# A merge moved behind the next unit's values, and two gate steps that work out of SBUF

## The chip, the cores and the metric

The kernel runs on one core of a Trainium2 chip. The metric is the device time of one execution in microseconds (us). The core's engines each work through a queue of their own: TensorE (PE in the profile, with PEld for its weight loads), VectorE (DVE), ScalarE (ACT), GpSimd (POOL) and SyncE (SP), which here only issues DMAs.

## The reference, cut to what matters

One layer of a decoder with 512 tokens, width 1024. One RMSNorm feeds one projection; half of its columns go to an attention with three branches (compressed blocks, selected blocks, window), half to a gated short convolution.

```python
h = rms_norm(x, norm_w); proj = h @ w_in
# attention, per block of 128 queries, 8 heads:
p_c = masked_softmax(q @ kc + bias);  o_c = p_c @ vc      # compressed keys, values
o_s = masked_softmax(q @ ks + bias) @ vs                  # selected blocks (here: all)
o_w = masked_softmax(q @ kw + bias) @ vw                  # window
attn = g0 * o_c + g1 * o_s + g2 * o_w
conv = conv_b * conv3(conv_c * conv_h)
mixed = concat([attn * silu(z_attn), conv * silu(z_conv)])
out = rms_norm(x + mixed @ w_out, final_norm_w)
```

## The kernel before, in words

Matrix products that need more than the engine's single pass split each operand into a high part and a rest and add three products (hi*hi, hi*lo, lo*hi). The high part of a weight is cast on ACT, the rest is subtracted on POOL.

**Order.** The order on TensorE is that of the program. ACT, DVE, POOL and the DMAs of SP are ordered by the compiler's planner, which takes what is ready in its own timeline; each engine then executes its queue strictly in that order. So the order on these four can change wherever the program changes.

**Units.** The attention is cut into 14 units: query blocks in the order 3, 2, 0, 1 (`BLOCKS`), each with two head groups (jj = 0, 1). A unit has `scores()` (products into the four PSUM banks `S`, L872; bias and maximum on DVE, L763; exponent on ACT, L881; weights on ACT L899 and DVE L900; a transposing DMA into `pt`, L902) and `values()` (L838 with `pt` and `V`, summed in a PSUM bank `o`, of which there are two). Block 0 has two units, 8 and 9, each with both the selected and the window branch; all others have one branch.

**The compressed branch.** Its scores are computed along with the first branch of each group (`fused`), its weights for all heads of a block at once in `Compressed.weigh()`, after the scores of the block's second group: DVE L807 to L814, POOL L818, ACT L819, POOL L820, and a transposing DMA into `ptc` (L822). `Group.merge()` adds the compressed branch to the group's bank `o` (L838 with `ptc`) and multiplies the bank into `za`, the gate (DVE L846).

**The loop.** In the loop at the end (L939 to L951) step n runs the values of unit n-2, the merge where its group is complete, the scores of unit n, and then fills TensorE with other tasks for a given cost (`st.fill`, 35 products of 512 columns, each counted as 216 ns, in the steps of blocks 0 and 1). At n = 10 all 27 projection tasks are completed first (`BEHIND`); behind them the fill consists of the product with the second half of the output matrix (`conv_out_task`: `pc`, L441 to L445, bank by bank `tb` in two PSUM banks `proj`, taken out by DVE L448) and of the casts and subtractions of the first half (`woa_task`, ACT L465, POOL L467).

**Gate chunks.** The projection tasks `za0` to `za3` and `zc0` to `zc3` end in `silu_to`: a multiplication by R in the PSUM bank (`normed`, DVE L274), a tanh on ACT (L281), a last step on DVE (L282), and for `zc` one more multiplication by R on POOL (L284). The bank is one of the two `proj` banks, 24 products fill it.

Of the kernel before, what the change touches and what calls it, by code (L numbers as in the profile page):

```python
# [9 lines left out]
F32 = mybir.dt.float32  # L10
# [3 lines left out]
AF = mybir.ActivationFunctionType  # L14
ALU = mybir.AluOpType
# [3 lines left out]
S = 512  # L19
# [67 lines left out]
def hybrid_kernel(ctx: ExitStack, tc: tile.TileContext, xt0, xt, x, ws, wt, wv, w1k, w1v, cst, rbr, wo, fnw, out):  # L87
    nc = tc.nc
    ctx.enter_context(tc.manual_schedule(engines={mybir.EngineType.PE}))
    one = ctx.enter_context(tc.tile_pool(name="one", bufs=1))  # L90
# [181 lines left out]
    def normed(ps):  # L272

        nc.vector.tensor_mul(ps, ps, R)  # L274
        return ps

    def silu_to(dst, conv=False):
        def evac(ps):

            normed(ps)  # L280
            nc.scalar.activation(dst(), ps, AF.Tanh, scale=0.5)  # L281
            nc.vector.scalar_tensor_tensor(out=dst(), in0=dst(), scalar=1.0, in1=ps, op0=ALU.add, op1=ALU.mult)  # L282
            if conv:
                nc.gpsimd.tensor_mul(dst(), dst(), R)  # L284
        return evac
# [305 lines left out]
    R = one.tile([128, S], F32, name="R")  # L591
# [68 lines left out]
    with tc.manual_schedule(engines={mybir.EngineType.Activation, mybir.EngineType.DVE, mybir.EngineType.Pool}):  # L660
# [4 lines left out]
        for k in range(8):  # L665
            if k % 2 == 0:
# [5 lines left out]
                                           op0=ALU.mult, op1=ALU.subtract)  # L672
# [241 lines left out]
    units, cmps = [], {qb: Compressed(qb) for qb in range(4)}  # L914
# [24 lines left out]
    for n in range(2, len(units) + 2):  # L939
        st.run(BEHIND.get(n, 0))  # L940
        u = units[n - 2]
        u.values()
        if 1 in u.brs:
            u.gr.merge()
        if n < len(units):
            units[n].scores()
            st.fill(FILL[units[n].gr.qb])
        elif n == len(units):

            st.run(len(st.tasks) - 2)  # L950
            st.fill(2700)  # L951
# [60 lines left out]
```

## Time and profile before

| what | before |
|---|---|
| time, median of 3 runs (lowest, highest) | 282.04 us (280.89, 282.22) |
| time of the profiled execution, its span | 282.41 us, 280.2 us |
| PE busy, PEld busy | 262.9 us (94%), 213.3 us (76%) |
| DVE, ACT, POOL busy | 180.7 us (65%), 151.6 us (54%), 145.2 us (52%) |
| mean granted TensorE clock | 0.976 |

The span runs from the first to the last instruction of one profiled execution; busy times are sums over the engine's instructions. The granted clock is the share of full speed that TensorE was given. All places in time are us from the start of the span. Idle time of an engine that nobody waits for costs nothing.

### The profile page before, as it was taken

The page shows a single profiled execution, that of the slowest core. Times are in us where ns is not written, and L with a number is a line of the kernel's source. Part 1 is how long each engine was busy: PE and PEld are TensorE (multiplying, and loading weights), DVE is VectorE, ACT ScalarE, POOL GpSimd, SP SyncE. Part 2 cuts the span into 40 slices and gives each one's busy share as a digit, 9 for nine tenths or more (in the row PEclk, how much of TensorE's full clock was granted, in tenths as well). Part 3 has the DMA queues.
Part 4 walks back from the last instruction along what each step waited for, and adds up shares of the span by engine and source line. Part 5 has one row for each costly group of instructions (what it writes and reads, how often), then busy time and mean ns, then how long its engine had stood idle before and what let it go on. Part 6 is the DMA issues. An engine that isn't in the chain of part 4 may idle for free. (4 is left out here: it accounts for less than half of the span.)

```text
span 280.2 us, 4423 instructions
## 1 busy us (share of the span) xinstructions
PE 262.9 (94%) x1488; PEld 213.3 (76%) x1488; DVE 180.7 (65%) x481; ACT 151.6 (54%) x342; POOL 145.2 (52%) x143
## 2 busy tenths in 40 slices
PE   7999999999999799999999999999990999999990
PEld 7888998878878578787878787878870867778780
DVE  5761937979766348663687854395990758758462
ACT  4973735577538356462727365538276516518542
POOL 5776596749341725636474947554648810005300
PEclk9999999999999999999999999999996699999997
DMA  6999997307944816947374688871929041352323
GB/s 200 392 287 271 211 220 273 106 0 219 198 185 88 195 57 148 210 102 196 80 160 102 152 229 206 202 210 20 207 51 253 34 78 37 75 152 39 112 102 122
DMA packets 57677, 43.29 MB, mean 155 GB/s; under 512 B 47288, under 2 KB 48568, under 8 KB 57656
## 3 DMA queue, kind: packets, MB, share of 16 engines
q1 hardware_dynamic: 57640, 43.03, 59.9%
q8 instruction: 11, 0.18, 0.2%
q14 instruction: 10, 0.08, 0.1%
q10 hardware_dynamic: 16, 0.00, 0.0%
HBM read 29.06 MB, written 2.42 MB: 112 GB/s over the span
## 5 line engine op out<-in xcount | busy, mean ns | idle before, releaser
L881 ACT ACTIVATE s<-s,mx 128x512 f32<-128x512 f32 (+3 forms) x64 | 32.0, 501 | 55.1 <-DVE mx L763 55.1
L763 DVE CUSTOM_DVE_ANT_0 s<-s,T 128x512 f32<-128x512 f32 (+3 forms) x64 | 29.7, 518 | 17.4 <-PE s L872 17.0
L900 DVE SCALAR_TENSOR_TENSOR p<-s,den,p 128x512 f16<-128x512 f32 (+3 forms) x64 | 32.2, 545 | 5.2 <-ACT p L899 4.7
L899 ACT ACTIVATE p<-s,den 128x512 f16<-128x512 f32 (+3 forms) x64 | 30.1, 537 | 6.6 <-issue 3.0
L872 PE MATMUL s<-K,Q 64*128 64x512 f32 (+5 forms) x168 | 19.2, 363 | 0.0
L254 POOL TENSOR_TENSOR wlob<-wrawb,whib 128x512 fp32r<-128x512 f32 x8 | 10.9, 1388 | 12.3 <-ACT whib L252 12.3
L254 POOL TENSOR_TENSOR wloh<-wrawh,whih 128x512 fp32r<-128x512 f32 x8 | 10.2, 1292 | 13.3 <-ACT whih L252 13.3
L254 POOL TENSOR_TENSOR wlozc<-wrawzc,whizc 128x512 fp32r<-128x512 f32 x8 | 10.1, 1283 | 13.5 <-ACT whizc L252 13.5
L872 PEld LDWEIGHTS s<-K,Q 64*128 64x128 f32 x168 | 13.9, 194 | 3.8 <-issue 2.3
L428 POOL TENSOR_TENSOR woclo<-wo,wochi 128x512 fp32r<-128x512 f32 x8 | 10.9, 1379 | 9.8 <-ACT wochi L426 9.8
L838 PEld LDWEIGHTS <-V 128*64 128x64 f16 x240 | 12.0, 109 | 5.0 <-issue 5.0
L838 PE MATMUL o<-pt,V 128*64 128x256 f16 x240 | 15.8, 275 | 0.0
L261 PE MATMUL psza<-hhi,whiza 128*128 128x512 f32 x32 | 12.8, 400 | 1.7 <-DVE za L282 1.7
L673 POOL TENSOR_TENSOR wlos<-wsr,whis 128x512 fp32r<-128x512 f32 x8 | 11.9, 1492 | 4.6 <-DVE whis L670 2.3
L254 POOL TENSOR_TENSOR wloq<-wrawq,whiq 128x512 fp32r<-128x512 f32 x8 | 10.2, 1292 | 7.9 <-ACT whiq L252 7.9
L441 PE MATMUL pc<-wochi,mc 128*128 128x512 f32 x32 | 13.4, 419 | 0.6 <-DVE y L448 0.6
L443 PE MATMUL pc<-woclo,mc 128*128 128x512 f32 x32 | 13.5, 422 | 0.0
L511 PE MATMUL po<-woa,mahi 128*128 128x512 f32 (+1 forms) x36 | 13.3, 369 | 0.0
L513 PE MATMUL po<-woa,mahi 128*128 128x512 f32 (+1 forms) x36 | 13.3, 369 | 0.0
L515 PE MATMUL po<-woa,malo 128*128 128x512 f32 (+1 forms) x36 | 13.3, 369 | 0.0
L445 PE MATMUL pc<-wochi,mc 128*128 128x512 f32 x32 | 13.3, 415 | 0.0
L881 ACT ACTIVATION_READ_ACCUMULATOR s<-s,mx 128x1 f32 x64 | 13.1, 205 | 0.0
(242 smaller groups left out, 810.6 us busy)
## 6 DMA issues: line engine op xcount, KB each, us to landing
wo<-in_wo SPq DMA_DIRECT2D x8, 512.0 KB, 3.7
wsr<-in_ws SPq DMA_DIRECT2D x8, 256.0 KB, 5.3
wrawq<-in_wt SPq DMA_DIRECT2D x4, 512.0 KB, 11.2
T<-vrd SPq DMA_DIRECT2D x8, 256.0 KB, 12.4
wrawza<-in_wt SPq DMA_DIRECT2D x4, 512.0 KB, 4.6
wrawzc<-in_wt SPq DMA_DIRECT2D x4, 512.0 KB, 3.8
wrawh<-in_wt SPq DMA_DIRECT2D x4, 512.0 KB, 4.0
wrawc<-in_wt SPq DMA_DIRECT2D x4, 512.0 KB, 3.4
```

Of the source, the lines that this page charges most:

```text
L254: nc.gpsimd.tensor_sub(lo[:, ks], t[:, ks], f32(hi[:, ks]))
L441: nc.tensor.matmul(ps, mc[0][:, 2 * kq + k, tsl], hi[:, k, :], start=(kq + k == 0), stop=False)
L443: nc.tensor.matmul(ps, mc[0][:, 2 * kq + k, tsl], lo[:, k, :], start=False, stop=False)
L445: nc.tensor.matmul(ps, mc[1][:, 2 * kq + k, tsl], hi[:, k, :], start=False, stop=last)
L511: nc.tensor.matmul(ps, mh[:, k, :], woa[0][:, k, ns], start=(k == 0), stop=False)
L513: nc.tensor.matmul(ps, mh[:, k, :], woa[1][:, k, ns], start=False, stop=False)
L763: nc.vector.tensor_tensor_reduce(out=dst, in0=src, in1=bias, scale=-1.0, scalar=3e38, op0=ALU.add, op1=ALU.min, accum_out=mx)
L838: nc.tensor.matmul(self.ob[ROWS[g], 0:256], v(g), p(g), start=(self.n_pv == 1), stop=(self.n_pv == 6 * (self.qb + 1) + 1))
L872: nc.tensor.matmul(s[g], q[ROWS[g], a, gr.qs], K[ROWS[g], b, brs[0]:brs[0] + nb, k0:k0 + W], start=(n == 0), stop=(n == 2))
L881: nc.scalar.activation(P[:, i], P[:, i], AF.Exp, bias=ngm, scale=-1.0, accum_out=self.su[:, i, j2, g:g + 1])
L899: nc.scalar.mul(p16[:, g, i, 0], P, c)
L900: nc.vector.scalar_tensor_tensor(out=p16[:, g, i, 1], in0=P, scalar=c, in1=p16[:, g, i, 0], op0=ALU.mult, op1=ALU.subtract)
```

## The change

`silu_to` no longer works in the PSUM bank: its first step (DVE) multiplies by R from the bank into the chunk's SBUF tile, the tanh (ACT) reads that tile and writes a new SBUF tile `th` (one buffer), and the last step (DVE) has both inputs in SBUF. In the loop, the merge of unit 8's group (block 0, jj = 0) no longer comes behind unit 8's values at n = 10 but at n = 11, behind unit 9's values and ahead of unit 9's own merge. All other merges stay where they were.

```diff
     def silu_to(dst, conv=False):
         def evac(ps):
 
-            normed(ps)
-            nc.scalar.activation(dst(), ps, AF.Tanh, scale=0.5)
-            nc.vector.scalar_tensor_tensor(out=dst(), in0=dst(), scalar=1.0, in1=ps, op0=ALU.add, op1=ALU.mult)
+            nc.vector.tensor_mul(dst(), ps, R)
+            th = one.tile([128, S], F32, tag="tanh", name="th")
+            nc.scalar.activation(th, dst(), AF.Tanh, scale=0.5)
+            nc.vector.scalar_tensor_tensor(out=dst(), in0=th, scalar=1.0, in1=dst(), op0=ALU.add, op1=ALU.mult)
             if conv:
                 nc.gpsimd.tensor_mul(dst(), dst(), R)
         return evac
@@
         u.values()
-        if 1 in u.brs:
+        if u.brs[0] == 1:
+            u.gr.merge()
+        elif u.gr.qb == 0 and u.gr.jj:
+
+            units[n - 3].gr.merge()
             u.gr.merge()
```

## Rows read from the trace of the kernel before

**Rows 1.** Page, section 2: granted clock in 40 slices of 7 us, in tenths.
```profile
PEclk9999999999999999999999999999996699999997
```
**Rows 2.** Waits of PE: who waited for whom, total us, times, longest.
```profile
PE o L838 <- DMA ptc<-pc: 7.1, 1, 7.1
PE psza L261 <- DVE za L282: 1.7, 1, 1.7
...
PE pc L441 <- DVE y L448: 0.6, 1, 0.6
```
**Rows 3.** Timeline of PE, 208 to 223: start, us, instruction, [idle before, releaser].
```profile
208.84 0.84 PE L838 MATMUL o<-pt,V 128*64 128x256 f16 x12
216.83 0.42 PE L838 MATMUL o<-ptc,vcs 128*64 128x256 f16 x2 [7.14 <-DMA ptc<-pc]
217.19 1.81 PE L872 MATMUL s<-K,Q 64*128 64x288 f32 x12
218.92 0.79 PE L443 MATMUL pc<-woclo,mc 128*128 128x512 f32 x1
219.51 0.63 PE L445 MATMUL pc<-wochi,mc 128*128 128x512 f32 x1
...
222.38 0.39 PE L441 MATMUL pc<-wochi,mc 128*128 128x512 f32 x1
```
**Rows 4.** Busy time by stretch: PE, PEld, DVE, ACT, POOL, then PEclk, DMA.
```profile
212.00:214.00 2.00, 0.00 (x0) 0.00 (x0) 0.00 (x0) 1.60 (x3) 2.00 (x3) 0.50 1.36 230
...
220.00:222.00 2.00, 2.00 (x6) 1.59 (x5) 1.70 (x9) 1.74 (x7) 1.57 (x2) 0.50 0.00 0
```
**Rows 5.** Chain that ended last, 230 to 232: start, us on the chain, what.
```profile
230.53 0.99 PE s L872 x11
231.52 0.43 PE pc L441
231.94 0.23 PE pc L443
```
**Rows 6.** Timeline of PE around the start of chunk za3.
```profile
90.85 0.39 PE L265 MATMUL psza<-hhi,wloza 128*128 128x512 f32 x1
92.98 0.50 PE L261 MATMUL psza<-hhi,whiza 128*128 128x512 f32 x1 [1.74 <-DVE za L282]
```
**Rows 7.** Timeline of DVE in the same place: first and last step of chunk za1.
```profile
90.89 0.69 DVE L274 TENSOR_TENSOR psza<-psza,R 128x512 f32<-128x512 f32 x1
92.24 0.69 DVE L282 SCALAR_TENSOR_TENSOR za<-za,psza 128x512 f32<-128x512 f32 x1 [0.66 <-ACT za L281]
```
**Rows 8.** Timeline of all engines, 196 to 201: one DVE form beside POOL and without.
```profile
196.59 2.73 POOL L428 TENSOR_TENSOR woclo<-wo,wochi 128x512 fp32r<-128x512 f32 x2
198.20 1.66 DVE L391 SCALAR_TENSOR_TENSOR ch<-cu,small,ch 128x512 f32<-128x512 f32 x1
200.18 0.73 DVE L391 SCALAR_TENSOR_TENSOR ch<-cu,small,ch 128x512 f32<-128x512 f32 x1
```
**Rows 9.** One line of the kernel, ACT from SBUF: ns min/median/max, first and last start.
```profile
L403 ACT CAST mc<-ch x4: 612/624/672, 165.3 to 213.0; 128x512 fp32r<-128x512 f32 x4
```
**Rows 10.** Timeline of DVE, 209 to 227.
```profile
209.78 0.68 DVE L402 TENSOR_TENSOR ch<-psb,ch 128x512 f32<-128x512 f32 x1
...
219.12 0.42 DVE L763 CUSTOM_DVE_ANT_0 s<-s,T 128x256 f32<-128x256 f32 x1
...
225.85 0.68 DVE L448 TENSOR_TENSOR y<-pc,y 128x512 f32<-128x512 f32 x1
```
**Rows 11.** Timeline of ACT, 214 to 220.
```profile
214.79 1.04 ACT L465 CAST woa<-wo 128x1024 fp32r<-128x1024 f32 x1 [1.20 <-DMA wo<-in_wo]
219.63 0.45 ACT L881 ACTIVATE s<-s,mx 128x256 f32<-128x256 f32 x1 [3.79 <-DVE mx L763]
```
**Rows 12.** Timeline of POOL, 211 to 226.
```profile
211.26 10.31 POOL L467 TENSOR_TENSOR woa<-wo,woa 128x512 fp32r<-128x512 f32 x8 [0.65 <-ACT woa L465]
222.49 2.55 POOL L428 TENSOR_TENSOR woclo<-wo,wochi 128x512 fp32r<-128x512 f32 x2 [0.92 <-ACT wochi L426]
```

## The prediction

> **What bounds the kernel now.** I read the page's busy shares first (the table of the profile has them): TensorE is busy for 262.9 of 280.2 us, every other engine for 65% at most. So the time is TensorE's work, plus its idle time, plus what a lowered clock adds. The clock slices show where to look: full speed throughout, except two slices at 0.6 from 210 us on, and the end [rows 1]. The waits of PE give the idle time that has a cause in the middle of the kernel: 7.1 us once for `ptc`, 1.7 us once for a gate chunk's bank, 0.6 us once for a bank of the output product [rows 2]. The change aims at the first two; nothing else in the list comes near them.
>
> The timeline shows the first place. Unit 8's values begin at 208.84 and take 0.84, to 209.68; the merge's two products start at 216.83, released by the DMA that writes `ptc`; then come unit 10's scores [rows 3]. TensorE did nothing for 7.14 us, and the granted clock fell to 0.50, the lower level of 1.2 GHz, from about 212 to 222, so also under work that follows the wait [rows 4].
>
> **The merge, moved.** What is removed is the wait: **7.14 us** [rows 3]. The same two products run one step later, at n = 11, and cost the same there.
>
> The clock comes back with it. At the low clock unit 10's scores took 218.92 - 217.19 = 1.73 us [rows 3]; the same twelve products of unit 11 take 0.99 at full clock [rows 5]: 0.74 saved. The next product took 219.51 - 218.92 = 0.59 against 0.43: 0.16. The seven behind it took 222.38 - 219.51 = 2.87, and at 0.233 each, which is the step at full clock [rows 5], they take 1.63: 1.24. Together **2.14 us**. The two products of the merge I leave out of this term.
>
> Is `ptc` there at the new place? It landed at 216.83 at the latest [rows 3]. TensorE reaches unit 10's scores at 209.68, and behind them come 35 products, of which unit 9's values and the merges follow: 209.68 + 0.99 + 0.43 + 34 x 0.233 + 0.84 = 219.9. That is 3.1 us after the landing, 1.7 us if TensorE comes 1.35 us earlier (next part) and the transfer does not. So the wait is covered by the fill, as long as the small steps in front of the DMA keep their place in POOL's queue.
>
> What is late next? The DVE instruction of the merge (L846) stood in DVE's queue during the wait, and everything behind it waited too; DVE was idle after L402, which ended at 210.46 [rows 10]. Without it the next user is TensorE itself: 23 of the 35 products fill the two banks `tb` 0 and 1, and the 24th needs the first bank back, which DVE L448 frees. Already before, this came 0.56 us late (the 0.6 of [rows 2]). That old wait goes out of the sum: **0.56 us**. In its place: TensorE wants the bank at 209.68 + 0.99 + 0.43 + 22 x 0.233 = 216.23. In the trace L448 stands behind unit 10's whole softmax in DVE's queue, and from its first L763 to the end of L448 it is 225.85 + 0.68 - 219.12 = 7.41 us [rows 10]. Started behind L402 at 210.46 the same queue frees the bank at 217.87, 1.6 us late. If the planner puts L448 in front of the softmax's last steps it is not late at all. Bounds 0 and 1.6 in this form; I take **1.4 us**, since the row with the same queue is the nearest, and TensorE is faster now than what the planner could count on.
>
> POOL's work in this stretch is 10.31 us of `woa` subtractions and then the pair for the last output task, done at 225.04 [rows 12]. That last task begins with the 13th product behind the fill of the next step: 219.9 + 0.99 + 0.43 + 23 x 0.233 = 226.7, so this pair is still in time by 1.6 us; it would cost what it slips beyond that, and I count nothing.
>
> **The gate chunks.** Chunk za3 needs the bank of za1. Its products could have started when za2's ended, at 91.24, and started at 92.98 [rows 6]: za1's first step ran from 90.89 to 91.58, its last one ended at 92.93 [rows 7]. With the change the bank is free after the first step, so with the same queue order za3 starts at 91.58 + 0.05 = 91.63 and **1.35 us** are saved. Bounds: all 1.74 if the planner brings the first step forward, 0 if it puts it later by the 1.35. It is the only chunk for which TensorE waited, so the other seven give nothing.
>
> The price of the steps: the first is a DVE pass from PSUM into SBUF, 0.68 as L402 [rows 10], against 0.69 [rows 7]; the tanh from SBUF 0.62 as L403 [rows 9], against less than the 0.66 between the steps [rows 7]. The last step now has both inputs in SBUF, as L391 has: 0.73 when POOL is quiet, 1.66 beside POOL's subtractions [rows 8], so +0.04 to +0.97 for each of eight, 7.8 us of DVE at most. All of it lies between 78 and 130 us beside TensorE's products; DVE is busy for 65% of the span (the table again), and PE waited for no bank of `S` there [rows 2]. I count nothing; what it costs without that cover is a rival below.
>
> **Sum**, from the profiled execution's 282.41: - 7.14 - 2.14 - 0.56 + 1.4 - 1.35 = - 9.79, so 272.6. The median of the runs shown is 0.37 below that execution, so the forecast for a median is **272.3 us**.
>
> **The rivals.**
>
> *The wait moves to ACT and DVE.* ACT's queue before held all four `woa` casts in front of unit 10's first exponent; the fourth waits for its DMA until 214.79 and ends at 215.83, the exponent ran at 219.63 [rows 11]. Kept in that order, the exponent starts at 215.83 instead, and from it to the end of L448 it is 226.53 - 219.63 = 6.90 us [rows 10, 11]. The bank is free at 222.7, TensorE restarts there and not at 226.59: 3.9 us won, less 2.14 if the clock falls again in the 6.5 us of waiting. With no gain left from the gate chunk that gives 278.5 to 280.6, some 279.3 in a median. For it: the queue of before. Against it: without the wait the scores are ready before the casts, and the planner takes what is ready.
>
> *The collision on SBUF.* The last steps of the chunks run up to 0.97 longer beside POOL [rows 8], and if DVE's lateness reached TensorE each time, 7 us would come back: 279.3. Against it: PE shows no wait for `S` at all. The Trainium skill ("SBUF — State Buffer", section "Who interferes with whom") says that a VectorE instruction with two SBUF inputs contends with a GpSimd instruction that reads SBUF and that the loser is blocked for the other's whole length; it speaks against this part of the change. The trace agrees in kind (1.66 against 0.73), and with an input in PSUM the step stayed at 0.69.
>
> *The wait for `ptc` only moves.* The three small steps in front of the transfer slip behind POOL's eight `woa` subtractions: 216.83 + 10.31 = 227.1, two merges (0.4) and the lost clock (2.14) make 229.7, against 230.53 where unit 11's scores began [rows 3, 5, 12]: 281.6, no change that can be told.
>
> *Slower.* One mechanism: these steps slip behind all ten POOL passes, 12.86 us [rows 12]. Then `ptc` lands at 229.7, and with 0.4 and 2.14 unit 11's scores stand at 232.2, 1.7 later than before: 284.1, or 283.7 in a median. It decides from 11.2 us of POOL work in front (230.53 - 2.14 - 0.4 - 216.83). Against it: in the trace the steps stand in front of the subtractions, and their inputs are ready first.
>
> **How the numbers follow.** Chances: the forecast 0.76, the ACT and DVE queue 0.13, the collision 0.03, `ptc` unchanged 0.05, slower 0.03. The forecast's own range goes from 270.5 (all of 7.14, 2.14, 0.56 and 1.74, no new wait) to 276 (no gain from the chunk, a new wait of 1.6 and the low clock's 2.14 with it). To leave out no more than 2 in 10 the range reaches into the ACT and DVE rival: 270.5 to 278. A measurement of this kernel can tell about 0.5%, 1.4 us, from no change. Faster by more: 0.76 + 0.13 + 0.03 = 0.92; within: 0.05; slower: 0.03.
>
> **What the changed profile would show.** Right: no wait for `ptc` in PE's list, full clock in the slices from 210 on, chunk za3 starting within 0.5 us of za2's end, a wait of 0 to 2 us of `pc` L441 for DVE L448 near 215, L282 at up to 1.66. Wrong: `o` L838 still waiting for `ptc` at n = 11 (the POOL rivals), a wait of over 3 us of `pc` with an exponent behind a `woa` cast (the ACT rival), or waits of `s` L872 for DVE between 78 and 130 (the collision).

## The result, and the profile after

| | before | after |
|---|---|---|
| time, median (lowest, highest) | 281.93 us of 4 (280.89, 282.22) | 274.14 us of 4 (272.69, 275.36) |
| profiled execution, its span | 282.41, 280.2 us | 274.34, 272.6 us |
| mean granted clock of it | 0.976 | 0.987 |

The ratio is 0.9728, 95% interval 0.9674 to 0.9782: faster by 2.2 to 3.3%. The forecast of 272.3 us lies 1.8 us below the median, inside its range of 270.5 to 278.0. The gain was named rightly; the price of the new wait was sized too low. An execution more than 1.5% above the fastest one of its kernel counts as slow and is in no median or ratio here: one of the short fill (277.85 us) and one of both orders (1458.71 us).

In the rows of the changed kernel the lines from L282 on stand one higher (L449 was L448, L882 was L881); of the gate chunk L280 is the first step, L282 the tanh, L283 the last. First the granted clock by slices and the waits of PE, to be read against [rows 1, 2]:

```profile
PEclk9999999999999999999999999999999979999997
```

```profile
PE pc L442 <- DVE y L449: 2.3, 1, 2.3
PE warm L665 <- DVE ones L148: 1.1, 1, 1.1
PE psza L261 <- DVE za L280: 0.5, 1, 0.5
```

The 7.1 us for `ptc` are gone, the gate chunk's 1.7 are 0.5, and the bank of the output product costs 2.3 instead of 0.6. One slice still shows a lower clock. The timeline of PE after the change, against [rows 3, 6] (three dots stand for lines left out):

```profile
90.53 0.39 PE L265 MATMUL psza<-hhi,wloza 128*128 128x512 f32 x1
91.42 0.50 PE L261 MATMUL psza<-hhi,whiza 128*128 128x512 f32 x1 [0.51 <-DVE za L280]
...
207.29 0.85 PE L839 MATMUL o<-pt,V 128*64 128x256 f16 x12
208.07 1.05 PE L873 MATMUL s<-K,Q 64*128 64x288 f32 x12
...
213.03 0.50 PE L446 MATMUL pc<-wochi,mc 128*128 128x512 f32 x1
...
214.54 0.40 PE L446 MATMUL pc<-wochi,mc 128*128 128x512 f32 x1
217.26 0.57 PE L442 MATMUL pc<-wochi,mc 128*128 128x512 f32 x1 [2.32 <-DVE y L449]
...
220.62 0.55 PE L446 MATMUL pc<-wochi,mc 128*128 128x512 f32 x1
...
222.46 0.39 PE L839 MATMUL o<-ptc,vcs 128*64 128x256 f16 x4
```

Unit 10's scores now follow unit 8's values directly. The 24th product behind them waits 2.32 us for its bank: the last product into that bank (`tb` 0) ended at 213.53, the last one into the other bank at 214.94, and then TensorE had nowhere to go on. Both merges (the four products at 222.46) wait for nothing. Busy time by stretch (PE, PEld, DVE, ACT, POOL, then the granted clock) shows what the new wait does to the clock, against [rows 4]:

```profile
216.00:217.00 1.00, 0.00 (x0) 0.00 (x0) 1.00 (x2) 1.00 (x3) 1.00 (x2) 1.00 0.00 0
217.00:218.00 1.00, 0.74 (x2) 0.63 (x3) 1.00 (x5) 1.00 (x3) 1.00 (x2) 0.77 0.00 0
218.00:219.00 1.00, 1.00 (x4) 0.75 (x3) 1.00 (x4) 0.20 (x1) 1.00 (x1) 0.50 0.06 16
```

It stood at 1.00 during the wait and fell to 0.50 (1.2 GHz) behind it, until about 221. Nine products from 217.26 to 221.01 took 3.75 us; at 0.233 each they take 2.10, so **1.65 us** went there.

What freed the bank late stands in the queues of DVE and ACT. DVE, 208 to 218, against [rows 10]:

```profile
208.82 0.42 DVE L764 CUSTOM_DVE_ANT_0 s<-s,T 128x256 f32<-128x256 f32 x1
...
212.24 0.73 DVE L405 TENSOR_TENSOR mc<-ch,mc 128x512 fp32r<-128x512 f32 x1 [1.79 <-ACT mc L404]
214.02 0.18 DVE L788 TENSOR_TENSOR pc<-s,T 128x15 f32<-128x15 f32 x1 [1.04 <-ACT s L882]
...
214.50 0.88 DVE L770 SCALAR_TENSOR_TENSOR den<-su,G 128x2 f32<-128x2 f32 x1
...
215.65 0.95 DVE L770 SCALAR_TENSOR_TENSOR den<-su,G 128x2 f32<-128x2 f32 x1
216.52 0.68 DVE L449 TENSOR_TENSOR y<-pc,y 128x512 f32<-128x512 f32 x1
```

ACT in the same stretch, against [rows 11]:

```profile
208.74 2.95 ACT L466 CAST woa<-wo 128x1024 fp32r<-128x1024 f32 x3
211.59 0.62 ACT L404 CAST mc<-ch 128x512 fp32r<-128x512 f32 x1
212.41 1.05 ACT L466 CAST woa<-wo 128x1024 fp32r<-128x1024 f32 x1 [0.19 <-DMA wo<-in_wo]
213.36 0.44 ACT L882 ACTIVATE s<-s,mx 128x256 f32<-128x256 f32 x1
```

The bank was complete at 213.53 and wanted back at 214.94. Its step L449 ran only at 216.52, because in DVE's queue it stood behind steps that need unit 10's exponents; the first exponent ran at 213.36, behind four `woa` casts and L404, though its maximum had been taken by about 209.3.

**Where the 8.07 us between the two profiled executions lie.** Up to the start of unit 8's values 1.55 (208.84 in [rows 3] against 207.29): 1.23 of it at chunk za3, 0.33 before 41 us (the first product of chunk `psq` began at 40.95 and at 40.62). From there to the end of the span 71.36 against 65.31, 6.05: 7.14 for `ptc` and 2.14 of clock won, 0.56 for the old bank wait, less 2.32 for the new and 1.65 for its clock, makes 5.87; 0.18 stay unassigned. Outside the span 2.21 against 1.74, 0.47. Together 8.07.

### The profile page after: what moved, and what is told of

It reads as the page before. It is cut to its first block, busy times and chain, and to the rows that moved or that the text cites. A ratio compares the mean times of both kernels' runs of the same rounds, so it can differ in the third digit from the quotient of the medians.

```text
span 272.6 us, 4425 instructions
## 1 busy us (share of the span) xinstructions
PE 262.0 (96%) x1488; PEld 212.0 (78%) x1488; DVE 183.4 (67%) x481; ACT 151.9 (56%) x342; POOL 147.9 (54%) x143
## 4 chain that ended last, share of the span: by engine, by line
PE 59%; issue 2%; DVE 2%; ACT 1%; POOL 1%; DMA 0%; POOLq 0%; DVEq 0%; ACTq 0%
PE o L839 6%; PE s L873 5%; PE psh L263 3%; PE psh L261 3%; PE psb L263 3%; PE psb L265 3%; PE pszc L265 3%; PE psh L265 3%; PE pszc L261 3%; PE psb L261 3%; PE psc L263 3%; PE psc L261 3%; PE pszc L263 3%; PE psc L265 3%; PE pc L442 3%
## 5 line engine op out<-in xcount | busy, mean ns | idle before, releaser
L882 ACT ACTIVATE s<-s,mx 128x512 f32<-128x512 f32 (+3 forms) x64 | 32.0, 501 | 48.6 <-DVE mx L764 48.5
L901 DVE SCALAR_TENSOR_TENSOR p<-s,den,p 128x512 f16<-128x512 f32 (+3 forms) x64 | 32.4, 544 | 5.0 <-ACT p L900 4.7
L873 PE MATMUL s<-K,Q 64*128 64x512 f32 (+5 forms) x168 | 18.5, 352 | 0.0
L254 POOL TENSOR_TENSOR wlozc<-wrawzc,whizc 128x512 fp32r<-128x512 f32 x8 | 11.4, 1456 | 10.9 <-ACT whizc L252 9.4
L873 PEld LDWEIGHTS s<-K,Q 64*128 64x128 f32 x168 | 13.3, 184 | 3.8 <-issue 2.1
L770 DVE SCALAR_TENSOR_TENSOR den<-su,G 128x2 f32<-128x2 f32 (+1 forms) x28 | 9.5, 338 | 5.5 <-ACT s L882 4.2
```

Of the source, the lines that this page charges most:

```text
L254: nc.gpsimd.tensor_sub(lo[:, ks], t[:, ks], f32(hi[:, ks]))
L873: nc.tensor.matmul(s[g], q[ROWS[g], a, gr.qs], K[ROWS[g], b, brs[0]:brs[0] + nb, k0:k0 + W], start=(n == 0), stop=(n == 2))
L882: nc.scalar.activation(P[:, i], P[:, i], AF.Exp, bias=ngm, scale=-1.0, accum_out=self.su[:, i, j2, g:g + 1])
L901: nc.vector.scalar_tensor_tensor(out=p16[:, g, i, 1], in0=P, scalar=c, in1=p16[:, g, i, 0], op0=ALU.mult, op1=ALU.subtract)
```

## The experiments

Theory: the two parts are worth what TensorE no longer waits for, and what is missing is the step L449 that comes late because of the order on DVE and ACT. Rivals: `ptc` has a thin cover that sets the time; the gate chunk's new step form costs TensorE something by the collision on SBUF; ACT's casts alone set the lateness.

**One part at a time.** The kernel before with the merge moved, and the kernel before with the new gate chunks (the two hunks of the change's diff, each alone).

> The merge of unit 8's group moved to n = 11 as in the change; the gate chunks as before. If the two parts act independently: the 7.1 us wait for ptc is gone, the wait of pc for L448 appears at 2 to 2.5 us with part of the clock's fall, chunk za3 still waits 1.7 us. Time 275 to 276 us, ratio 0.975 to 0.980. If the gate part were what made room for the transfer, the wait for ptc would still be in PE's list at n = 11 and the time above 279.

> The gate chunks as in the change, the merge at its old place. The wait of za3 falls from 1.7 to about 0.5 us; TensorE comes 1.2 us earlier to unit 8's values, and so do the scores that ptc hangs on, so the wait for ptc stays at about 7. Time 280.8 us, ratio 0.9955. If the transfer's time is set by a load that does not follow TensorE, the wait for ptc grows to 8.3 and the ratio is 1.000. If the last gate step's collision with POOL reaches TensorE, waits of s L872 for DVE appear between 78 and 130 and the ratio is above 1.00.

The merge alone: 277.16 us (274.52 to 278.17), ratio 0.9801 [0.9719, 0.9884]: faster, but not clearly by 2%, and slower than the 275 to 276 expected. The gate chunks alone: 280.30 us (279.34 to 280.84), ratio 0.9923 [0.9899, 0.9947]: a gain clear of no change but under 2%, and a little more than expected (280.8). The waits of PE with the merge alone:

```profile
PE pc L441 <- DVE y L448: 2.4, 1, 2.4
PE psza L261 <- DVE za L282: 1.7, 1, 1.7
```

and with the gate chunks alone:

```profile
PE o L839 <- DMA ptc<-pc: 7.1, 1, 7.1
PE psza L261 <- DVE za L280: 0.5, 1, 0.5
PE pc L442 <- DVE y L449: 0.4, 1, 0.4
```

Each part takes away its own wait and leaves the other's as it was. The new bank wait belongs to the merge (2.4 without the new chunks). With the new chunks alone no wait for a score bank appears between 78 and 130 us, so the collision does not reach TensorE there. The gate part gives 1.65 us in the median; the merge alone gives 4.8, a loose number, since its four executions spread by 3.65 us. Together that is 6.4 against the 7.8 of the whole change, a gap that lies within this spread.

**ACT's order.** The changed kernel and the kernel before, each with the `woa` casts held behind `behind["u"]`, ACT's last weights step of the latest unit (only the cast is shown; `behind["u"]` is set where that step is issued):

```
-            nc.scalar.copy(hi, t)
+            with tc.issue_after(behind["u"]):
+                nc.scalar.copy(hi, t)
```

> The changed kernel, with the four woa casts held behind the last weight step of the latest unit in ACT's queue. Theory ACT queue: unit 10's first exponent starts at about 209.5 and not at 213.4, the bank of tb 0 is free some 1 to 3 us earlier, the wait of pc for L449 falls from 2.3 to 1.1 us or less and the clock does not fall; 270.5 to 272.3 us, ratio 0.960 to 0.966. Theory DVE order (L449 is late because it stands behind the whole softmax on DVE, whatever ACT does): wait and time as in the changed kernel, ratio 0.973.

> The kernel before, with the woa casts held behind as in the run above. Theory ACT queue as the second bound only: the wait for ptc stays at 7.1 us, the bank wait of 0.6 goes, ratio 0.997 to 1.000: ACT's queue bounds nothing until the merge is moved. If the casts also delay the transfer of ptc, its wait falls below 5 and the ratio below 0.99.

In the changed kernel, 272.20 us (272.15 to 272.61), ratio 0.9639 [0.9596, 0.9681], 2 us below the change as it stands. In the kernel before, 282.19 us, ratio 0.9999 [0.9970, 1.0029]: no gain, with the wait for `ptc` still at 7.0. Waits of PE, then ACT and DVE, in the changed kernel with this order (lines one higher again):

```profile
PE pc L442 <- DVE T L449: 1.1, 1, 1.1
PE pc L442 <- DVE y L449: 0.7, 1, 0.7
```

```profile
210.78 0.45 ACT L883 ACTIVATE s<-s,mx 128x256 f32<-128x256 f32 x1 [1.16 <-DVE mx L765]
```

```profile
214.69 0.68 DVE L449 TENSOR_TENSOR y<-pc,y 128x512 f32<-128x512 f32 x1
```

The exponent runs as soon as its maximum is there, at 210.78 instead of 213.36, L449 at 214.69 instead of 216.52, the wait is 0.7 instead of 2.3, and the clock keeps 0.9 in every slice until the last. A part comes back: with the casts late, the cast of `wochi` waits for its DMA in front of unit 11's exponents, and the second group's bank (`T`) costs 1.1. The order was worth nothing before, when the same stretch was idle.

**Is ACT's lateness all of it?** Only the third and fourth cast held behind (the same edit under `if i < 2`):

> The changed kernel with only the third and fourth woa cast held behind the unit's last weight step; the first two stay in front of unit 10's exponents on ACT. Theory ACT queue: each cast in front costs 1 us, and the fourth also its wait for a load; so the first exponent lies between 209.5 and 213.4, near 211.5, the bank wait between 0.7 and 2.3, near 1.2, and the clock holds; 272.0 to 273.0 us, ratio 0.964 to 0.968. Theory DVE order: as the changed kernel, 0.973.

273.98 us (273.35 to 275.39), ratio 0.9716 [0.9670, 0.9761]: as the change itself, against what my theory of ACT's queue expected (272.0 to 273.0) and as the rival, the order on DVE, had it. The first exponent was early, at 211.00. DVE of this kernel:

```profile
211.12 1.68 DVE L405 TENSOR_TENSOR mc<-ch,mc 128x512 fp32r<-128x512 f32 x1 [1.61 <-ACT mc L404]
...
215.33 1.66 DVE L902 SCALAR_TENSOR_TENSOR p<-s,den,p 128x256 f16<-128x256 f32 x4
216.90 0.68 DVE L449 TENSOR_TENSOR y<-pc,y 128x512 f32<-128x512 f32 x1
```

The planner put L405 (1.61 us of waiting and 1.68 of work) between the maxima, and L449 behind all four weights steps; the wait was 2.9, and the clock fell behind it. So the early exponent alone does not do it: what counts is everything that stands in front of one DVE step.

**The DVE step itself.** The changed kernel, with unit 10's compressed scores and weights on DVE put off into `held` and issued behind L449 of the first group, `behind["y"]`; ACT as it was (only the loop is shown; the rest of the 35 products of fill follows behind the held steps):

```
-            units[n].scores()
+            held = [] if n == 10 else None
+            units[n].scores(held)
+            if held:
+                st.fill(17 * 216)
+                with tc.issue_after(behind["y"]):
+                    for step in held:
+                        step()
```

> The changed kernel; on DVE the step that takes out the bank of tb 0 (L449) is put ahead of the compressed scores and the weights of unit 10, ACT's queue stays with all four casts in front. Theory DVE order: the bank is free near 214.5, its wait goes to under 0.5 us, no fall of the clock, 270.5 to 272 us (0.960 to 0.965), though ACT is as late as in the changed kernel. Theory ACT queue alone: the softmax stays late and holds the S banks, so unit 11's scores wait 1 us or more instead, 272.5 to 274 (0.967 to 0.972).

272.05 us (271.68 to 272.48), ratio 0.9645 [0.9618, 0.9671]. ACT and DVE:

```profile
213.72 0.44 ACT L882 ACTIVATE s<-s,mx 128x256 f32<-128x256 f32 x1
```

```profile
213.12 0.69 DVE L449 TENSOR_TENSOR y<-pc,y 128x512 f32<-128x512 f32 x1 [0.59 <-PE pc L446]
```

The exponents are as late as in the changed kernel (213.72), and the wait for `y` is gone, the lower clock with it: L449 now waits for TensorE. This separates the two causes. ACT's lateness mattered because L449 stood behind it.

**How thin is the cover of `ptc`?** The changed kernel with 23 instead of 35 products of fill at n = 10 (`st.fill(... if n != 10 else 23 * 216)`), and with unit 8's merge at n = 10, behind 14 products of fill.

> The changed kernel, the fill of step n = 10 cut from 35 to 23 products, so that the product which needs the late bank comes behind unit 9's values, the merges and unit 11's scores. If the bank is all that is late, its wait goes and the time falls to 271 us (0.961). If unit 10's softmax as a whole is late, unit 11's scores wait instead for the S banks that it holds, about 1.5 to 2.5 us from 216 on, and the time stays at 273 to 274.5 (0.969 to 0.973). The transfer of ptc is then needed at about 215.7 and not at 222.5; a wait for it shows when it landed.

> The changed kernel, but unit 8's merge stands at n = 10 behind unit 10's scores and 14 products of the fill, so TensorE reaches it near 212.5 and not near 222.5. If ptc lands near 214.3 (issue at 209.9, 4.4 to landing): a wait of 1.8 us for ptc, and the bank wait that follows is shorter by as much, so 273.5 to 274.5 (0.970 to 0.973): half the cover would have done nearly as well. If the landing is near 216.8 less 1.5, as the kernel before had it: a wait of about 2.8, the clock falls, 275 to 276.5 (0.975 to 0.981).

The short fill: 274.82 us (273.19 to 276.09, three executions), ratio 0.9738 [0.9684, 0.9792]. Merge within the fill: 274.35 us (273.08 to 274.61), ratio 0.9717 [0.9684, 0.9749]. PE's waits with the short fill, then PE's timeline with the merge within the fill:

```profile
PE s L873 <- DVE p L901: 2.2, 2, 1.9
```

```profile
215.09 0.30 PE L839 MATMUL o<-ptc,vcs 128*64 128x256 f16 x2 [2.65 <-DMA ptc<-pc]
```

With the short fill the merges come at 215.46 and still wait for nothing, so `ptc` had landed; within the fill they start at 215.09, released by it. It lands near 215.0 in this kernel, which issues it at 210.13; the changed kernel issues it at 209.92 and uses it at 222.46. That is about 7.4 us of cover, or 3.5 without the 2.32 us of the bank wait and the 1.65 us of clock behind it (an estimate, with the landing taken from the other kernel). The rival of the thin cover falls. The short fill takes the bank wait away and gets 1.9 us of waiting for a score bank in its place, released by unit 10's weights (L901): TensorE meets the same late softmax elsewhere, and the clock falls to 0.50 there too, from about 220.1 to 223.5. The merge within the fill waits longer than the change (2.6 and 1.1) and takes the same time. Of its two expected outcomes it has the wait of the second and the time of the first, because the clock did not fall behind 2.65 us of waiting:

```profile
PEclk9999999999999999999999999999999999999996
```

**Both orders at once.** The casts are held behind and L449 comes first. This kernel was run twice, because the profiled execution of the first run was stretched (last section); the L449 order alone was run again beside it.

> The changed kernel with both orders at once: the casts of woa behind unit 10's exponents on ScalarE, and the step that frees the compressed branch's first bank (y<-pc,y of the first group) ahead of unit 10's compressed scores and weights on VectorE. Theory (the bank wait is set by what stands in front of that one VectorE step; either order alone already takes it to 0.7 us or less, and what is left of each, a wait of 0.8 to 1.1 us of the second group's bank, has other causes): no further gain worth speaking of, 271.5 to 272.3 us, ratio 0.962 to 0.966, the wait of y at the first group gone. Rival (the lateness of the exponents costs a second wait of its own, which e8 only hid): another 1 us, 270.5 to 271.2 us, ratio 0.958 to 0.961.

> The kernel with both orders once more, since its profiled execution came out at 1458 us with all of TensorE's matmuls stretched and shows nothing of the orders. Theory (the two orders overlap, a wait of the second group's bank of about 0.8 us and the 0.5 us at 91 us stay): 272 to 272.7 us, no wait of y at the first group's bank, no later wait of more than 1.2 us. Rival (the two orders get into each other's way: the wochi cast's wait on its DMA now holds unit 10's weights): a wait of 0.5 to 1.5 us of TensorE on probabilities or score banks of units 10 or 11, 272.6 to 273.4 us.

> The kernel with VectorE's bank step first, on the same chip as the one with both orders. Theory: 271.7 to 272.5 us again, within 0.5 us of the one with both orders. Rival (both orders get into each other's way): 0.5 to 1.2 us faster than the one with both orders.

Both orders: 272.59 us (median of the five executions of 272.10 to 273.46), 0.3 above the expected range, and 272.58 (272.39 to 272.90), ratio 0.9665 both times [0.9640, 0.9690] and [0.9641, 0.9689]. L449 first alone: 272.28 (271.74 to 272.50), ratio 0.9648 [0.9627, 0.9670]. No further gain: each order removes the same wait. Waits of PE with both:

```profile
PE psza L261 <- DVE za L280: 0.5, 1, 0.5
PE pk_vc L686 <- DVE whis L672: 0.4, 1, 0.4
PE pc L442 <- DVE T L449: 0.8, 1, 0.8
PE s L874 <- DVE p L907: 0.6, 1, 0.6
```

The 0.6 for unit 10's weights is the cast of `wochi` in front of them, as the rival said; 0.3 us between the two is too little to be told.

**The gate part again, where nothing blurs it.** The kernel before with the merge moved and L449 first, but the old gate chunks.

> The kernel before with the merge moved and with VectorE's bank step first, but with its old gate chunks: the changed kernel's gate part undone where no bank wait and no lower clock blur the number. Theory (the gate part takes 1.2 to 1.35 us from TensorE's wait on za's banks near 91 us and nothing else): that wait is 1.7 us again, the time 1.2 to 1.7 us above e8's 272.05 us, 273.2 to 273.8 us, ratio 0.969 to 0.972. Rival (the gate part's gain is hidden later by the fixed order on the other engines once the bank wait is gone): as e8, 272.0 to 272.5 us, ratio 0.964 to 0.966.

274.07 us (273.94 to 274.21), ratio 0.9711 [0.9687, 0.9735]; with the new chunks 272.05 and 272.28. So the gate part is worth 1.8 to 2.0 us here, over the theory's upper end of 1.7. From the first product of `psza` to the second one of za3 it is 23.44 us with the old chunks (69.83 to 93.27) and 22.21 with the new (69.11 to 91.32): 1.23, the wait and no more. The rest is there before the chunks: the first product of `psq` began at 40.84 to 41.09 in the four kernels with old chunks whose traces I have and at 40.18 to 40.65 in the nine with new ones. No gate chunk runs there. In this pair of traces the difference arises in the kernel's first products, old chunks and then new:

```profile
5.78 0.63 PE L684 MATMUL pk_kc<-hhi,whis 128*128 128x512 f32 x1
6.20 0.63 PE L684 MATMUL pk_ks<-hhi,whis 128*128 128x512 f32 x1
```

```profile
5.47 0.39 PE L685 MATMUL pk_kc<-hhi,whis 128*128 128x512 f32 x1
5.70 0.40 PE L685 MATMUL pk_ks<-hhi,whis 128*128 128x512 f32 x1
```

With the old chunks the first five follow each other by 0.40 to 0.57 us, up to 7.03, with the new ones by 0.23 from 5.47 on, and the ninth product is 0.87 us apart. But the kernel before with the casts held behind also begins with the short step and still reaches `psq` only at 40.84. So no run ties this remainder to the chunks; it is open.

## Why the prediction was right, and where it was off

**The wait for `ptc`, 7.14: right.** It went whole, and nothing took its place there. The cover of 3.1 us was sized about rightly: `ptc` lands near 215.0 and not 216.83, mostly because the whole kernel is 1.55 us earlier by then, and its use at 222.46 holds 2.32 us of new wait and 1.65 us of clock, without which 3.5 us of cover are left.

**The clock, 2.14: right as a gain, wrong as a net.** The old loss went, but 1.65 us were lost again behind the new wait, a net of 0.49. My sum took a wait of 1.4 us and full clock behind it; the low clock behind a new wait stood only in the range's end. This is the largest error, 1.65.

**The new bank wait, 1.4: mis-sized, 2.32.** Its upper bound of 1.6 did not hold. The step that failed is the 7.41 us from the first maximum to the end of L448, taken over from [rows 10]. After, it is 217.20 - 208.82 = 8.38. I had started the old queue earlier and asked only what DVE needs; in the old trace the exponent followed its maximum by 0.51 us (219.12 to 219.63, [rows 10, 11]), after the `woa` casts had long been done. Moved up by 10 us the same queue meets the casts: 4.54 us from the first maximum to the first exponent (208.82 to 213.36). The planner's new order gave 3.06 of these 4.03 us back: from the exponent to the end of L449 it is 3.84 us and not 6.90. About 1.85 of that is L449 standing ahead of the four weights steps, 0.93 the cast of `wochi` no longer standing between the third and the fourth exponent, the rest a maximum that they no longer wait for. That the term was only 0.9 short is luck: two larger errors nearly cancelled. The start at 210.46 also left out a step that stood ahead of the first maximum in the old queue (L404, 1.50 us); after, it stands behind the maxima (L405, 212.24) and ends before the exponent, so it cost nothing. The ACT rival had this mechanism right, the exponent right behind the fourth cast, and a wrong size, 6.5 of waiting. The forecast and this rival were not exclusive: with the exponent at 213.36 and the bank wanted at 214.94, the old 6.90 gives a wait of 5.3 and the 3.84 measured gives 2.3.

**The gate chunk, 1.35: right, 1.23.** DVE after, against [rows 7]:

```profile
90.69 0.68 DVE L280 TENSOR_TENSOR za<-psza,R 128x512 f32<-128x512 f32 x1
92.07 0.69 DVE L283 SCALAR_TENSOR_TENSOR za<-th,za 128x512 f32<-128x512 f32 x1 [0.70 <-ACT th L282]
```

The bank is free at 91.37 and za3 starts at 91.42. In the median the part is worth 1.65 to 2.0, 0.4 to 0.8 more than this wait, which is not explained.

**The collision on SBUF: there, and rightly priced at nothing at the chunks.** The last step of the chunks, against the 0.69 of [rows 7] and the 0.73 and 1.66 of [rows 8], and a two-column step of the softmax:

```profile
L283 DVE SCALAR_TENSOR_TENSOR za<-th,za x4: 672/846/1587, 78.2 to 104.8; 128x512 f32<-128x512 f32 x4
L283 DVE SCALAR_TENSOR_TENSOR zc<-th,zc x4: 1198/1330/1527, 108.8 to 127.0; 128x512 f32<-128x512 f32 x4
```

```profile
L770 DVE SCALAR_TENSOR_TENSOR den<-su,G x28: 149/158/1323, 62.7 to 246.2; 128x2 f32<-128x2 f32 x24, 128x4 f32<-128x4 f32 x4
```

Up to 1.59 us, within the bound of 1.66, and no wait of TensorE follows from it. But the L770 steps right ahead of L449 took 0.88 and 0.95 us where such a step takes 0.158 in the median, beside POOL's `woa` subtractions, 1.5 us more. The fourth exponent ended only at 215.28, so some 1.0 of the 8.38 hangs on it (an estimate from these rows). Such steps stood in the old queue too, at 0.77 and 0.80, so my 7.41 held them unseen. The Trainium skill ("SBUF — State Buffer", section "Who interferes with whom") has the loser blocked for the other's whole instruction; the trace agrees as far as these small steps go, whose longest, 1.32 at 65.76, stood beside POOL's `wloza` subtractions (6.27 us for five, 1.25 each). With the casts held behind, POOL does nothing from 209.13 to 215.19 and the two steps take 0.16 each; with L449 first, beside the subtractions, they take 0.15 and 0.43, so they are not hit every time. No run took this loss away by itself.

**The sum.** Forecast 272.6 for a profiled execution, measured 274.34: + 1.65 clock, + 0.92 bank wait, + 0.12 gate chunk, - 0.33 before 41 us, - 0.18 unassigned, - 0.47 outside the span, together 1.71, the 1.74 up to rounding. The slower and the `ptc` rivals did not come about: POOL's steps kept their place in front of the subtractions.

## What to carry to other kernels

When a wait is taken away, don't move the old queue up as a block: redraw it with the new times, since steps that had been done for long (casts in front of an exponent) now stand in front of what is needed first. Ask of each step that frees a PSUM bank what stands ahead of it on its own engine, and which other engine those steps wait for; putting that one step first was worth 2 us here, as much as reordering the other engine. A new wait is to be priced with the clock that may fall behind it, which here cost 1.65 us on top of 2.32 in the traced execution; but it need not fall, as the 2.65 us of waiting within the fill show.

## What was not expected of the hardware

Waits of like length did not lower the clock alike. In the traces it fell to 0.50 behind 2.32 us (the change), 2.4 us (the merge alone) and 2.9 us (two casts behind), and in the short fill behind two waits of 1.88 and 0.36 us; it stayed at 1.00 behind 2.65 us (the merge within the fill), and the 1.74 us before za3 [rows 6] never lowered it in a trace I have. What decides it is not shown here.

Whether it falls every time in one and the same kernel is not shown either, since only the profiled executions have a trace. The four executions of the changed kernel took 274.34, 273.94, 275.36 and 272.69 us at mean granted clocks of 0.987, 0.986, 0.986 and 0.992, a spread of 2.7 us. The fastest also has the highest clock, which fits a fall that stayed away or was shorter; the second and third differ by 1.4 us at the same clock. Kernels without this wait spread by 0.3 to 0.8 us at 0.992 to 0.998 (casts behind, L449 first, L449 first without the gate part), and by 0.5 and 1.4 us at 0.990 to 0.997 (both orders).

One execution, the profiled one of the kernel with both orders, took 1458.71 us; the other five took 272.10 to 273.46. Its page shows every product stretched:

```profile
L263 PE MATMUL psh<-hlo,whih 128*128 128x512 f32 x32 | 54.6, 1705 | 0.0
```

A product of 512 columns took 1.7 us instead of 0.39, at a recorded mean clock of 1.0. It is left out of every comparison here, and its cause is open.
